# Bias tables loaded during the mixer instead of at the start of attention, and the first head's tiles in other space, in a hybrid attention and RWKV layer

## Chip, cores and metric

The kernel runs on one core of one Trainium2 chip. The metric is device microseconds of one execution. The core has a matrix engine (TensorE, PE in the profile, with its weight loads as PEld), VectorE (DVE), ScalarE (ACT), GpSimd (POOL) and SyncE (SP), and 16 DMA engines that move data between HBM and the on-chip memories SBUF (128 partitions) and PSUM. DMAs are issued by an engine's queue: SPq, ACTq or POOLq in the rows.

## What is computed

One layer of a trunk over 2048 tokens of width 1024. Three token mixers read columns of one projection of the normalised input: A is attention in chunks of 64 frames with a learned relative-position bias (4 heads), B is forgetting attention (4 heads), C is an RWKV-7 recurrence (8 heads). Their outputs are concatenated, projected and added; a gated feed-forward network follows. The part that the change touches is A:

```python
rel = kj - LEFT_CHUNKS * CHUNK - qi
bias = rel_table[:, jnp.clip(rel, -MAX_REL, MAX_REL) + MAX_REL].astype(jnp.float32)
...
    s = jnp.einsum('bhqd,bhkd->bhqk', qc, kb).astype(jnp.float32) + bias
    s = jnp.where(valid, s, NEG_INF)
    p = jax.nn.softmax(s, axis=-1).astype(vb.dtype)
    return jnp.einsum('bhqk,bhkd->bhqd', p, vb)
```

## The kernel before

The work runs in stages, one behind the other: the mixer (0 to about 1195 us), attention A and B (to about 1620 us), the output projection, and the feed-forward network (to 3254 us).

**The mixer** goes over four blocks of 512 tokens (`b` in `range(NB)`), each in four steps `i`. `project` multiplies the normalised input, whose tiles are `hT`, with slices of the weights (lines 268 to 270); `rwkv_front`, `rwkv_inverse` and `rwkv_back` compute the recurrence and are woven with it by generators. The inverse is a run of short VectorE instructions on `T` and `tm` (lines 520, 523), followed by small transfers through DRAM (`iD`, `E`, `DT`) on SP's queue. The recurrence reads `LZ` and the running state `S` in matmuls at lines 639 and 640. Queries and keys are written to `qkD` in DRAM as two halves `qh` and `ql` (lines 691, 692). For each block the last step of the recurrence loads `bv` (line 667), GpSimd adds it to `yl` (line 668), VectorE adds a PSUM tile (line 671), and GpSimd issues the store to `yD`. During block 1, `bias_rows` writes the relative biases, spread out, to `extD` and `exttD` in DRAM.

**Attention** goes over units: one head and one block of 512 queries. `shift` finds each query's largest score: for each of the four 128-query tiles matmuls write the scores to the PSUM tile `s` (lines 982, 987; there is one such tile), VectorE adds the bias table `TS` and takes the maximum (`sj`, line 991, with the read of the maximum as a second row), the four maxima are transposed (line 1012), and written into rows of `Q2` (line 1013). `attend` then computes transposed scores `st` with two matmuls (line 1043 with `Q1`, line 1044 with `Q2`, which needs the maxima), adds the table `TR` (line 1052), takes the exponential (line 1055) and multiplies with the values (line 1061). The shifts of units 0 and 1 stand ahead of the first `attend`; from then on the shift of unit u+2 is woven into `attend` of unit u.

`head` issues the loads of keys (`K1`, `K2`, lines 942 to 944) and values (`VA`, line 950) on SP, `queries` those of the queries (lines 959 to 961), for the first four units on ACT's queue (`QQ`). `bias` prepares the two tables of one head. It stands at the start of attention, and its loads are issued on ACT's queue (`BQ`), `TS` at line 904 and `TR` at line 906. Two constant tiles are made there too: `caub`, a cast of the loaded `cauf`, and `nid`.

The order in which an engine works is fixed when the program is built: a scheduler merges the generators' instructions for each engine, and an engine does not step past an instruction that waits. Each DMA on the queues of SP and ACT takes the next of eight completion counters, `DMAHW0` to `DMAHW7`, in turn, and is issued only when the DMA eight places earlier, which had the same counter, has landed.

Space in SBUF is given out by pools, as stacks from the left and from the right (`side="right"`). A tile that lies where an earlier stage's tile lay waits for that tile's last reader. Before, the right side begins with `hTp` (the `hT` tiles), then `xtp`, and after the mixer with `hd0` (head 0's keys), `qp` and `sm`, so the first keys lie over `hT`.

Of the kernel before, what the change touches and what calls it, by code (L numbers as in the profile page):

```python
# [48 lines left out]
PSB = {"m": 3, "f": 2, "b": 2}  # L49
# [48 lines left out]
def trunk_kernel(ctx: ExitStack, tc: tile.TileContext, xT, w_in, pp, cst, cau, rel, relr, w2, a2, g2, w_out, w_up, w_down, out, dbg=None):  # L98
# [39 lines left out]

    def copy(e, out, in_):
        e.copy(out, in_) if e is nc.scalar else e.tensor_copy(out=out, in_=in_)  # L140
# [6 lines left out]
    p1 = ExitStack()  # L147
    hTp = p1.enter_context(tc.tile_pool(name="hTp", bufs=1, side="right"))
    xtp = p1.enter_context(tc.tile_pool(name="xtp", bufs=1, side="right"))
# [6 lines left out]
    lzp = p1.enter_context(tc.tile_pool(name="lzp", bufs=NR0))  # L156
# [20 lines left out]
    nc.sync.dma_start(out=cst1, in_=cst[:, 256:NCC])  # L177

# [663 lines left out]
    for b in range(NB):  # L842
# [4 lines left out]
        for i in range(4):  # L847
            res = {}
            if b == 0 and i == 0:
                late.pop()()  # L850
                weave((), fill(b, hT, PRE))
            fills[:] = [fill(b, hT, jobs[i])]
            weave(
                (back, inv),
                lora_in(hT, lo) if i == 0 and b else (),
                rwkv_front(b, i, hT, lo, res),
                prepare(b + 1, xs) if i == 2 and b + 1 < NB else (),
                fills[0],
            )
            back, inv = (rwkv_back(prev) if prev else None), rwkv_inverse(res)  # L860
            prev = res
            if b == 1 and i == 1:
                bias_rows()
    weave((back, inv), fill(b, hT, LAST[4]))
# [8 lines left out]
    hd0 = p2.enter_context(tc.tile_pool(name="hd0", bufs=1, side="right"))  # L873
    qp = p2.enter_context(tc.tile_pool(name="qp", bufs=1, side="right"))
    sm = p2.enter_context(tc.tile_pool(name="sm", bufs=3, side="right"))
# [6 lines left out]
    cA = pA.enter_context(tc.tile_pool(name="cA", bufs=1, side="right"))  # L882
# [14 lines left out]

    TS = cA.tile([P, 4, 640], F32, name="TS")
    TR = cA.tile([P, 4, 256], F32, name="TR")

    def bias(h, q):

        a = extD[h].rearrange("q j -> (q j)")[127 : 127 + P * (EXT - 1)]
        q.dma_start(out=TS[:, h, :], in_=a.rearrange("(q j) -> q j", q=P)[:, 0:640])
        a = exttD[h].rearrange("q j -> (q j)")[127 : 127 + P * (EXTT - 1)]
        q.dma_start(out=TR[:, h, :], in_=a.rearrange("(q j) -> q j", q=P)[:, 0:256])
        nc.gpsimd.memset(TS[0:64, h, 576:640], NEG)
        nc.gpsimd.memset(TS[64:128, h, 0:64], NEG)
        nc.vector.tensor_scalar(TR[:, h, :], TR[:, h, :], par("rel0", h), None, op0=ALU.subtract)
        nc.gpsimd.memset(TR[64:128, h, 0:64], NEG)  # L910


    NQ = 4
    KVs, Qs = [], []
    for r, hd in enumerate((hd0, hd1)):
# [5 lines left out]
        nc.gpsimd.memset(f(K2[64:68, :]), 1.0)  # L921
        nc.gpsimd.memset(VA[:, :, 64:128], 1.0)
        nc.gpsimd.memset(f(V[:, :, 64:128]), 1.0)
        KVs.append((K1, K2, VA, V, VL))
    for r in range(NQ):
        Q1 = qp.tile([P, TB], F32R, name=f"Q1{r}")
        Q2 = qp.tile([70, TB], F32R, name=f"Q2{r}")
        QM = qp.tile([70, TB], F32R, name=f"QM{r}")
        for q in (Q2, QM):
            nc.gpsimd.memset(f(q[64:70, :]), 1.0)  # L930
        nc.gpsimd.memset(f(QM[64:68, :]), 0.0)
        Qs.append((Q1, Q2, QM))
# [89 lines left out]
    nid = c2.tile([4, 4, 1], F32, name="nid")  # L1022
    nc.vector.tensor_scalar(nid[:, :, 0], ident[0:4, 0:4], -1.0, None, op0=ALU.mult)
# [82 lines left out]
    bias(0, BQ(nc))  # L1106
# [8 lines left out]
    for h in range(1, 4):  # L1115
        bias(h, BQ(nc))
# [347 lines left out]
```

## Time and profile before

| what | us |
|---|---|
| median of 3 runs | 3266.54 |
| the 3 runs | 3254.4, 3266.54, 3267.34 |
| profiled execution | 3256.01 |
| its span, first to last instruction | 3254.2 |

The profiled execution is one run with the profiler on; rows below are from it, and their times count from its first instruction. PE is busy 93% of the span. PEclk is the granted clock of TensorE as a share of its full speed of 2.4 GHz, so 0.50 is 1.2 GHz. "DMA share" is the mean busy share of the 16 DMA engines (it can pass 1 in a short window, since packets are counted where they end). In brackets at the end of a timeline row stands how long the engine sat idle before it and what ended that.

### The profile page before, as it was taken

What the parts mean: (1) busy time and instruction counts of PE and PEld (TensorE: products, weight loads), DVE (VectorE), ACT (ScalarE), POOL (GpSimd) and SP (SyncE); (2) the same over time, 40 slices, a digit from 0 to 9 for tenths busy, and PEclk for the clock granted to TensorE, in tenths of its full rate; (3) what the DMA queues carried; (4) which work ended last, traced back from release to release, by engine and by line L of the source; (5) the groups of instructions that cost most, each with busy time, mean ns of one, the idle gap of its engine ahead of it and who ended that gap; (6) DMA issues with size and microseconds to landing.
All of it is one profiled execution on the core that took longest, in us unless ns stands there. A gap on an engine that the chain in (4) does not pass through costs nothing.

```text
span 3254.2 us, 49317 instructions
## 1 busy us (share of the span) xinstructions
PE 3037.6 (93%) x17820; PEld 2650.9 (81%) x17820; DVE 2373.9 (73%) x4569; ACT 1399.3 (43%) x2610; POOL 1000.3 (31%) x949
## 2 busy tenths in 40 slices
PE   6888899999999979999999999999899999999999
PEld 4567777776777755667699899999799998899999
DVE  5666666766677645677644688889988889988886
ACT  5343444434444334578733333333333334333332
POOL 3221001001000020144433444444544444444442
PEclk8888899999999987999999999999999999999999
DMA  7555665655653565532224422222422222422221
GB/s 222 148 166 170 175 181 163 190 149 157 162 161 101 169 152 141 141 99 77 76 90 148 143 79 78 78 78 74 154 74 77 78 78 81 140 78 78 78 79 67
DMA packets 440228, 392.94 MB, mean 121 GB/s; under 512 B 138809, under 2 KB 365637, under 8 KB 438633
## 3 DMA queue, kind: packets, MB, share of 16 engines
q1 hardware_dynamic: 435056, 377.99, 39.7%
q0 software_dynamic: 2816, 8.39, 0.9%
q10 hardware_dynamic: 2112, 3.41, 0.5%
q8 instruction: 141, 2.31, 0.3%
q14 instruction: 103, 0.84, 0.1%
HBM read 304.65 MB, written 86.36 MB: 120 GB/s over the span
## 4 chain that ended last, share of the span: by engine, by line
PE 66%; DVE 18%; issue 5%; ACT 4%; DMA 4%; POOL 2%; SPq 1%; POOLq 0%; ACTq 0%; DVEq 0%
PE ps L1291 7%; PE ps L1290 7%; PE ps L1289 7%; PE ps L1337 4%; PE ps L1335 4%; PE ps L1336 4%; PE mm L268 3%; PE mm L270 3%; PE mm L269 3%; DVE T L523 2%; PE o L1061 2%; DVE tm L520 2%; DVE wu L144 2%; PE z L639 2%; PE ps L1197 2%
## 5 line engine op out<-in xcount | busy, mean ns | idle before, releaser
L1291 PE MATMUL ps<-B,wu 128*128 128x340 f32 (+1 forms) x1848 | 593.2, 321 | 20.0 <-DVE wu L144 20.0
L1290 PE MATMUL ps<-B,wu 128*128 128x340 f32 (+1 forms) x1848 | 592.0, 320 | 0.0
L1289 PE MATMUL ps<-B,wu 128*128 128x340 f32 (+1 forms) x1848 | 589.4, 319 | 2.5 <-ACT wu L143 1.7
L1291 PEld LDWEIGHTS ps<-B,wu 128*128 128x128 f32 x1848 | 348.0, 188 | 27.6 <-DVE wu L144 27.2
L1335 PE MATMUL ps<-hid,wd 128*128 128x340 f32 (+1 forms) x1056 | 342.1, 324 | 14.3 <-ACT wd L143 10.2
L1289 PEld LDWEIGHTS ps<-B,wu 128*128 128x128 f32 x1848 | 347.9, 188 | 3.2 <-ACT wu L143 2.0
L1290 PEld LDWEIGHTS ps<-B,wu 128*128 128x128 f32 x1848 | 348.6, 189 | 0.1
L1337 PE MATMUL ps<-hid,wd 128*128 128x340 f32 (+1 forms) x1056 | 339.9, 323 | 3.1 <-POOL wd L144 3.0
L1336 PE MATMUL ps<-hid,wd 128*128 128x340 f32 (+1 forms) x1056 | 339.9, 322 | 0.0
L144 DVE TENSOR_TENSOR wu<-S,wu 128x512 fp32r<-128x512 f32 x264 | 257.0, 978 | 74.7 <-ACT wu L143 74.7
L1338 DVE TENSOR_TENSOR acc<-acc,ps 128x340 f32<-128x340 f32 (+1 forms) x528 | 248.3, 503 | 52.9 <-PE ps L1337 52.2
L144 POOL TENSOR_TENSOR wd<-raw,wd 128x1024 fp32r<-128x1024 f32 x66 | 171.0, 2613 | 277.3 <-ACT wd L143 272.9
L268 PE MATMUL mm<-hT,whi 128*128 128x512 f32 x520 | 235.9, 454 | 18.0 <-ACT whi L143 12.8
L270 PE MATMUL mm<-hT,wlo 128*128 128x512 f32 x520 | 220.3, 424 | 10.4 <-POOL wlo L144 6.4
L143 ACT CAST wu<-S 128x512 fp32r<-128x512 f32 x264 | 163.1, 619 | 150.5 <-PE ps L1291 137.9
L269 PE MATMUL mm<-hT,whi 128*128 128x512 f32 x520 | 219.3, 422 | 4.9 <-DVE hT L144 3.9
L1335 PEld LDWEIGHTS ps<-hid,wd 128*128 128x128 f32 x1056 | 201.8, 191 | 18.0 <-ACT wd L143 11.0
L144 DVE TENSOR_TENSOR wu<-raw,wu 128x512 fp32r<-128x512 f32 x198 | 203.0, 1026 | 6.4 <-ACT wu L143 6.4
L1337 PEld LDWEIGHTS ps<-hid,wd 128*128 128x128 f32 x1056 | 200.2, 190 | 5.5 <-POOL wd L144 5.5
L1336 PEld LDWEIGHTS ps<-hid,wd 128*128 128x128 f32 x1056 | 201.2, 190 | 0.0
L143 ACT CAST wu<-raw 128x512 fp32r<-128x512 f32 x198 | 121.5, 620 | 165.3 <-PE ps L1291 147.4
L268 PEld LDWEIGHTS mm<-hT,whi 128*128 128x128 f32 x520 | 105.5, 203 | 49.5 <-ACT whi L143 13.6
(348 smaller groups left out, 7140.4 us busy)
## 6 DMA issues: line engine op xcount, KB each, us to landing
raw<-in_w_up_dram SPq DMA_DIRECT2D x132, 512.0 KB
raw<-in_w_down_dram SPq DMA_DIRECT2D x66, 512.0 KB
whi<-whiD SPq DMA_DIRECT2D x48, 512.0 KB
wlo<-wloD SPq DMA_DIRECT2D x48, 512.0 KB
wraw<-in_w_in_dram SPq DMA_DIRECT2D x24, 512.0 KB
whiD<-whi SPq DMA_DIRECT2D x24, 512.0 KB
wloD<-wlo SPq DMA_DIRECT2D x24, 512.0 KB
xt<-in_xT_dram SPq DMA_DIRECT2D x48, 256.0 KB
```

The lines of the kernel that those rows point to most:

```text
L143: (hi_eng or nc.scalar).copy(hi, src) if (hi_eng or nc.scalar) is nc.scalar else hi_eng.tensor_copy(out=hi, in_=src)
L144: (lo_eng or nc.vector).tensor_tensor(lo, src, f(hi), op=ALU.subtract)
L268: mm(ps, hi[:, kt, 0:P], hT[kt][:, 0, :], start=(kt == 0), stop=False)
L269: mm(ps, hi[:, kt, 0:P], hT[kt][:, 1, :], start=False, stop=False)
L270: mm(ps, lo[:, kt, 0:P], hT[kt][:, 0, :], start=False, stop=(kt == KT - 1))
L1289: mm(ps, whl[:, 0, kt, :], Bs[p][:, kt, 0, 0:n], start=(kt == 0), stop=False)
L1290: mm(ps, whl[:, 0, kt, :], Bs[p][:, kt, 1, 0:n], start=False, stop=False)
L1291: mm(ps, whl[:, 1, kt, :], Bs[p][:, kt, 0, 0:n], start=False, stop=(kt == 3))
L1335: mm(ps, wd[:, 0, ch], hid[:, 0, cs], start=(u == 0), stop=False)
L1336: mm(ps, wd[:, 0, ch], hid[:, 1, cs], start=False, stop=False)
L1337: mm(ps, wd[:, 1, ch], hid[:, 0, cs], start=False, stop=(u == G - 1))
L1338: nc.vector.tensor_tensor(acc[ct][:, cs], acc[ct][:, cs], ps, op=ALU.add)
```

## The change

`bias` and its two tables move up. The tables lie in a pool `cA` that exists for the whole kernel, and `bias(i, nc.sync)` runs at the end of each step of block 2, so that its two loads for head `i` are issued on SP's queue, its memsets on GpSimd and its subtraction on VectorE somewhere during that block. The space (4 x 896 floats, 14,336 bytes in each partition) comes out of the scratch memory for DMA descriptors, which shrinks from its default of 16,384 to 2,048 bytes. The right side now begins with `xtp` and `lzp` (the `LZ` tiles), so head 0's keys and the queries lie over those; `hT` comes third, and `va` and `prA` lie over it. The PSUM pools of the mixer are opened in another order. GpSimd's memsets of ones are reordered, with those that the first units don't read in a function `ones`. `nid` is made at the start.

```diff
-PSB = {"m": 3, "f": 2, "b": 2}
+PSB = {"f": 2, "m": 3, "b": 2}
...
+    cA = ctx.enter_context(tc.tile_pool(name="cA", bufs=1))
+    TS = cA.tile([P, 4, 640], F32, name="TS")
+    TR = cA.tile([P, 4, 256], F32, name="TR")
+    nid = const.tile([4, 4, 1], F32, name="nid")
+
+    def bias(h, q):
+
+        a = extD[h].rearrange("q j -> (q j)")[127 : 127 + P * (EXT - 1)]
+        q.dma_start(out=TS[:, h, :], in_=a.rearrange("(q j) -> q j", q=P)[:, 0:640])
+        a = exttD[h].rearrange("q j -> (q j)")[127 : 127 + P * (EXTT - 1)]
+        q.dma_start(out=TR[:, h, :], in_=a.rearrange("(q j) -> q j", q=P)[:, 0:256])
+        nc.gpsimd.memset(TS[0:64, h, 576:640], NEG)
+        nc.gpsimd.memset(TS[64:128, h, 0:64], NEG)
+        nc.vector.tensor_scalar(TR[:, h, :], TR[:, h, :], par("rel0", h), None, op0=ALU.subtract)
+        nc.gpsimd.memset(TR[64:128, h, 0:64], NEG)
...
+    xtp = p1.enter_context(tc.tile_pool(name="xtp", bufs=1, side="right"))
+    lzp = p1.enter_context(tc.tile_pool(name="lzp", bufs=NR0, side="right"))
     hTp = p1.enter_context(tc.tile_pool(name="hTp", bufs=1, side="right"))
-    xtp = p1.enter_context(tc.tile_pool(name="xtp", bufs=1, side="right"))
...
-    lzp = p1.enter_context(tc.tile_pool(name="lzp", bufs=NR0))
...
                 bias_rows()
+            if b == 2:
+                bias(i, nc.sync)
...
     hd0 = p2.enter_context(tc.tile_pool(name="hd0", bufs=1, side="right"))
+    sm = p2.enter_context(tc.tile_pool(name="sm", bufs=3, side="right"))
     qp = p2.enter_context(tc.tile_pool(name="qp", bufs=1, side="right"))
-    sm = p2.enter_context(tc.tile_pool(name="sm", bufs=3, side="right"))
...
-    cA = pA.enter_context(tc.tile_pool(name="cA", bufs=1, side="right"))
...
-        Qs.append((Q1, Q2, QM))
+        Qs.insert(0, (Q1, Q2, QM))
+    nc.gpsimd.memset(f(KVs[0][1][64:68, :]), 1.0)
+    for Q1, Q2, QM in Qs:
+        nc.gpsimd.memset(f(Q2[64:70, :]), 1.0)
+    nc.gpsimd.memset(KVs[0][2][:, :, 64:128], 1.0)
+
+    def ones():
+        nc.gpsimd.memset(f(KVs[1][1][64:68, :]), 1.0)
...
-    bias(0, BQ(nc))
...
-    for h in range(1, 4):
-        bias(h, BQ(nc))
+    ones()
...
-    nc = _bacc.Bacc("TRN2", target_bir_lowering=False, num_devices=1)
+    nc = _bacc.Bacc("TRN2", target_bir_lowering=False, num_devices=1, dynamic_dma_scratch_size=2048)
```

Lines of the mixer move by 20 with the change, those of attention by 11 to 21 (the keys' loads 942 to 944 are 955 to 957, the values' 950 is 963, `sj` 991 is 1004, `st` 1043 and 1044 are 1054 and 1055; `TS` and `TR` 904 and 906 are 149 and 151).

**SP's queue at the end of the mixer.** This is the queue from the last store of the mixer's forget gates (`ckD`) on. A wait on `DMAHW` is one for an earlier DMA, one on `PE` for the last matmul that read the tile below. Before:

```order
L748 DMA ckD<-cl 4x512 [waits DMAHW0_49,DVE_49]
L691 DMA qkD<-qh 128x512 [waits DMAHW1_49,Activation_49]
L692 DMA qkD<-ql 128x512 [waits DMAHW2_49,DVE_49]
L942 DMA K_11077<-qkD 64x512 [waits DMAHW4_49,PE_49]
L943 DMA K_11077<-qkD 64x512 [waits DMAHW6_49]
L944 DMA K_11078<-qkD 64x512 [waits DMAHW7_49]
L942 DMA K_11077<-qkD 64x512 [waits DMAHW1_49]
L943 DMA K_11077<-qkD 64x512 [waits DMAHW2_49]
L667 DMA bv<-bD 128x512 [waits DVE_49,DMAHW4_49,PE_49,Pool_49]
L893 DMA cauf<-in_cau_dram 128x256 [waits DMAHW5_49,DVE_49,PE_49]
```

and of the change, from the same store (five more `DMA` rows stand between it and `bv` than before):

```order
L955 DMA K_11103<-qkD 64x512 [waits DMAHW4_49]
L956 DMA K_11103<-qkD 64x512 [waits DMAHW5_49]
L711 DMA qkD<-qh 128x512 [waits DMAHW6_49,Activation_49]
L712 DMA qkD<-ql 128x512 [waits DMAHW7_49,DVE_49]
L963 DMA VA_11105<-vA 128x4x64 [waits DMAHW1_49,PE_49]
L957 DMA K_11104<-qkD 64x512 [waits DMAHW3_49]
L963 DMA VA_11105<-vA 128x4x64 [waits DMAHW4_49]
L955 DMA K_11103<-qkD 64x512 [waits DMAHW6_49]
L956 DMA K_11103<-qkD 64x512 [waits DMAHW7_49]
L687 DMA bv<-bD 128x512 [waits DVE_49,DMAHW1_49,PE_49,Pool_49]
L914 DMA cauf<-in_cau_dram 128x256 [waits DMAHW2_49,DVE_49,PE_49]
```

The five loads of head 0's first keys (the last two of them are the first rows here) have moved ahead of the last stores of `qh` and `ql`, and their `PE` wait is for the last matmul that reads `LZ` instead of the last that reads `hT`. Two loads of values and three more of keys have moved ahead of `bv`. The `DMAHW1` that `bv` waits for is the counter of the first `VA`.

**VectorE at the same place.** Before, from the end of the mixer to the second unit's shift:

```order
L894 CAST caub<-cauf 128x256 [waits DMAHW5_49]
L909 TENSOR_SCALAR TR<-TR,pps 128x256 [waits DMAHW7_49,DMAHW2_49]
L671 TENSOR_TENSOR yl<-yl,rw 128x512 [waits DMASW6_49,Pool_49]
L991 ISA sj,M<-s,TS 128x128 [waits DMAHW3_49,PE_49,Pool_49]
...
L1013 SCALAR_TENSOR_TENSOR Q_11094<-s,pps,nid 4x512 [waits PE_49]
L909 TENSOR_SCALAR TR<-TR,pps 128x256 [waits DMAHW5_49]
L991 ISA sj,M<-s,TS 128x640 [waits DVE_49,PE_49,Pool_49]
```

and of the change:

```order
L1004 ISA sj,M<-s,TS 128x384 [waits PE_49]
L1004 ISA M 128x1
L162 TENSOR_TENSOR ql<-rn,qh 128x512 [waits DMAHW6_49,DMAHW7_49,DMAHW3_49,Activation_49]
L1004 ISA sj,M<-s,TS 128x512 [waits PE_49]
L1004 ISA M 128x1
L1026 SCALAR_TENSOR_TENSOR Q_11123<-s,pps,nid 4x512 [waits PE_49,Pool_49]
L691 TENSOR_TENSOR yl<-yl,rw 128x512 [waits DMASW6_49,Pool_49]
L915 CAST caub<-cauf 128x256 [waits DMAHW2_49]
L1004 ISA sj,M<-s,TS 128x640 [waits DVE_49,PE_49]
```

The first shift (`sj` up to the write of `Q`) has moved ahead of `yl` and `caub`, and `sj` no longer waits for the load of a table or for GpSimd's memsets on it. The second shift still stands behind `yl`, which waits for GpSimd's sum with `bv`, and `caub`.

**SP's queue in block 2 of the mixer.** Of the change, with the loads of the inverse (`iD`) at the end:

```order
L271 DMA wraw<-whiD_512_2401 128x4x256 [waits DMAHW1_49,PE_49]
L151 DMA TR<-exttD 128x256 [waits DMAHW2_49]
L149 DMA TS<-extD 128x640 [waits DMAHW3_49]
L271 DMA whi<-whiD_2564_605 128x8x128 [waits DMAHW4_49,PE_49]
...
L149 DMA TS<-extD 128x640 [waits DMAHW3_49]
L151 DMA TR<-exttD 128x256 [waits DMAHW4_49]
L149 DMA TS<-extD 128x640 [waits DMAHW5_49]
L548 DMA iD<-T 256x1x32 [waits DMAHW6_49,DVE_49,Pool_49]
```

Here six of the eight new loads stand between the weights' loads, one `TS` stands earlier and one `TR` later; before, none stood there. On VectorE the first subtraction on `TR` (line 154) stands within the run of `T` and `tm`:

```order
L543 TENSOR_TENSOR T<-T,tm 128x5x15 [waits DVE_49]
L154 TENSOR_SCALAR TR<-TR,pps 128x256 [waits DMAHW2_49]
L540 TENSOR_TENSOR tm<-T,NT 128x70 [waits DVE_49]
```

It waits for the `TR` load of the row above, and all of VectorE's later work stands behind it.

## Rows read from the trace of the kernel before

**Rows 1.** The page of before: section 1, busy us of the engines.
```profile
PE 3037.6 (93%) x17820; PEld 2650.9 (81%) x17820; DVE 2373.9 (73%) x4569; ACT 1399.3 (43%) x2610; POOL 1000.3 (31%) x949
```
**Rows 2.** Windows, mixer's end: busy us by engine, PEclk, DMA share, GB/s.
```profile
1180.00:1190.00 10.00, 9.82 (x52) 7.42 (x51) 5.71 (x13) 4.14 (x9) 0.00 (x0) 1.00 0.02 5
...
1200.00:1205.00 5.00, 0.00 (x0) 0.00 (x0) 0.76 (x1) 0.00 (x0) 2.12 (x2) 0.50 1.06 258
...
1220.00:1225.00 5.00, 3.06 (x5) 1.19 (x6) 3.21 (x9) 1.36 (x3) 0.44 (x3) 0.50 1.08 224
...
1240.00:1245.00 5.00, 5.00 (x14) 3.25 (x13) 1.34 (x5) 1.50 (x5) 0.29 (x2) 0.50 0.00 0
```
**Rows 3.** The chain that ended last: start us, us, what.
```profile
1192.16 3.35 DMA qkD<-ql
...
1195.53 7.26 DMA K<-qkD
...
1219.98 9.06 DMA TR<-exttD
```
**Rows 4.** DMA view of 1185 to 1245 us: packets; issues, KB each.
```profile
DMA packets 8730, 9.87 MB, mean 164 GB/s; under 512 B 4916, under 2 KB 5556, under 8 KB 8536
...
TS<-extD ACTq DMA_DIRECT2D x4, 320.0 KB
...
TR<-exttD ACTq DMA_DIRECT2D x4, 128.0 KB
```
**Rows 5.** Timeline, 1186 to 1235 us: start, us, instruction, [idle before].
```profile
1186.62 0.62 PE L639 MATMUL z<-UV,LZ 128*128 128x64 f32 x4
...
1192.63 0.57 SPq L942 DMA_DIRECT2D K<-qkD  x1
...
1196.47 0.33 SPq L667 DMA_DIRECT2D bv<-bD  x1
...
1203.82 1.25 POOL L668 TENSOR_TENSOR yl<-yl,bv 128x512 f32<-128x512 f32 x1 [2.88 <-DMA bv<-bD]
...
1204.24 0.98 DVE L894 CAST caub<-cauf 128x256 bf16<-128x256 f32 x1 [7.01 <-DMA cauf<-in_cau_dram]
...
1206.18 0.67 DVE L671 TENSOR_TENSOR yl<-yl,rw 128x512 f32<-128x512 f32 x1
...
1210.63 0.14 POOL L907 MEMSET TS<- 64x64 f32 x1
1210.81 0.29 DVE L991 CUSTOM_DVE_ANT_0 sj<-s,TS 128x128 bf16<-128x128 f32 x1 [3.96 <-POOL TS L907]
...
1215.60 0.74 DVE L1013 SCALAR_TENSOR_TENSOR Q<-s,pps,nid 4x512 fp32r<-4x512 f32 x1 [0.47 <-PE s L1012]
...
1220.89 0.82 DVE L991 CUSTOM_DVE_ANT_0 sj<-s,TS 128x640 bf16<-128x640 f32 x1
...
1222.70 0.82 DVE L991 CUSTOM_DVE_ANT_0 sj<-s,TS 128x640 bf16<-128x640 f32 x1 [0.32 <-PE s L987]
...
1231.14 0.82 DVE L991 CUSTOM_DVE_ANT_0 sj<-s,TS 128x640 bf16<-128x640 f32 x1 [0.78 <-PE s L987]
...
1234.13 1.54 PE L1044 MATMUL st<-Q,K 68*128 68x512 f32 x4
```
**Rows 6.** Windows in the mixer, 620 to 660 us: columns as in group 2.
```profile
620.00:640.00 20.00, 18.57 (x129) 13.88 (x128) 15.40 (x53) 8.20 (x16) 0.00 (x0) 0.91 0.89 250
640.00:660.00 20.00, 19.04 (x93) 14.37 (x92) 15.05 (x56) 14.81 (x28) 0.73 (x5) 1.00 0.63 175
```
**Rows 7.** Timeline of the mixer: SyncE's queue and VectorE.
```profile
639.71 0.52 SPq L251 DMA_DIRECT2D whi<-whiD  x1
...
643.86 0.23 DVE L523 TENSOR_TENSOR T<-T,tm 128x70 f32<-128x70 f32 x1
```
**Rows 8.** Line L909 and line L1093, each from its own view.
```profile
L909 DVE TENSOR_SCALAR TR<-TR,pps x4: 349/353/1112, 1205.1 to 1229.1; 128x256 f32<-128x256 f32 x4
...
DMA to landing us min/median/max: 2.2/2.3/7.8
```

More of the change, by code (lines that the diff above doesn't have):

```diff
@@ L177, in trunk_kernel @@
     nc.sync.dma_start(out=cst1, in_=cst[:, 256:NCC])
+    nc.vector.tensor_scalar(nid[:, :, 0], ident[0:4, 0:4], -1.0, None, op0=ALU.mult)
     omu = c1.tile([P, 14], F32, name="omu")
@@ L894, in trunk_kernel @@
     nc.vector.tensor_copy(out=caub, in_=cauf)
[L898 to L910, printed above, removed]
     NQ = 4
@@ L920, in trunk_kernel @@
         VL = vb.tile([P, 16, 64], F32R, name=f"VL{r}")
-        nc.gpsimd.memset(f(K2[64:68, :]), 1.0)
-        nc.gpsimd.memset(VA[:, :, 64:128], 1.0)
-        nc.gpsimd.memset(f(V[:, :, 64:128]), 1.0)
         KVs.append((K1, K2, VA, V, VL))
@@ L928, in trunk_kernel @@
         QM = qp.tile([70, TB], F32R, name=f"QM{r}")
-        for q in (Q2, QM):
-            nc.gpsimd.memset(f(q[64:70, :]), 1.0)
-        nc.gpsimd.memset(f(QM[64:68, :]), 0.0)
-        Qs.append((Q1, Q2, QM))
+        Qs.insert(0, (Q1, Q2, QM))
[5 more added lines that the diff above has]
+        nc.gpsimd.memset(f(KVs[1][1][64:68, :]), 1.0)
+        nc.gpsimd.memset(KVs[1][2][:, :, 64:128], 1.0)
+        for Q1, Q2, QM in Qs:
+            nc.gpsimd.memset(f(QM[64:70, :]), 1.0)
+            nc.gpsimd.memset(f(QM[64:68, :]), 0.0)
+        for K1, K2, VA, V, VL in KVs:
+            nc.gpsimd.memset(f(V[:, :, 64:128]), 1.0)
     def head(n, c=0, parts=1):
@@ L1020, in shift @@
         )
-    nid = c2.tile([4, 4, 1], F32, name="nid")
-    nc.vector.tensor_scalar(nid[:, :, 0], ident[0:4, 0:4], -1.0, None, op0=ALU.mult)
     pending = collections.deque()
```

## The prediction

> **What bounds the kernel now.** The page comes first: PE is busy 3037.6 us, 93% of the span of 3254.2 [rows 1], so a change that leaves the matrix work as it is can win only from PE's idle time, 217 us in all. The windows show where a piece of it lies. Until 1190 us PE is busy 9.82 of 10 us; in 1200 to 1205 it does nothing, in 1220 to 1225 it works 3.06 of 5, and all of that at a granted clock of 0.50, which it still has in 1240 to 1245 [rows 2]. This is the passage from the mixer to attention. The DMA engines were idle before it (share 0.02) and full in it (1.06 to 1.08, 258 and 224 GB/s). The chain of waits says for what: a store of queries (3.35 us), keys (7.26 us), and last a `TR` table (9.06 us) [rows 3]. The DMA view gives its size: 9.87 MB in the passage, of which the bias tables are 4 x (320 + 128) KB = 1.83 MB [rows 4].
>
> The timeline shows how the engines hang on it [rows 5]. The first `sj` (1210.81) sat idle 3.96 us for GpSimd's memset on a `TS` table. The second shift runs from 1220.89; its last `sj` starts at 1231.14, though its first two are only 1.81 us apart, because a `TR` subtraction stands ahead on VectorE and its load is late. The first `st` matmul on the second unit's maxima starts at 1234.13. I take this matmul as the anchor: behind it the change leaves the work as it is, so the gain is what the anchor moves, less what the mixer pays.
>
> **The passage, worked out.** Three things are removed there: 1.83 MB of loads, the memsets, and four subtractions on VectorE, one of 1.11 us and the others near 0.35 [rows 8]. One thing moves: head 0's keys are now requested when the last matmul on `LZ` has ended, 1186.62 + 0.62 = 1187.2, instead of at 1192.63 [rows 5]. That alone does not start attention sooner, since the queries' load stays where it was on ACT's queue, beside the store at 1192.16. A lightly loaded transfer takes 3.35 us [rows 3], so the first shift can start near 1195.5. From the first `sj` to its write of `Q` it took 1210.81 to 1215.60 + 0.74, or 5.5 us; with four VectorE instructions of the mixer between, each taken like `yl` at 0.67, it ends near 1203.7.
>
> Then `yl` and `caub` are next on VectorE, and here a new order costs something. `bv` was issued at 1196.47 and GpSimd could use it at 1203.82, 7.35 us later. Now it stands behind the first `VA`, on whose counter it waits. That load goes out behind the store at 1192.16, near 1192.6. No row shows a 128 KB value load in such a lull; it takes between 3.35 and 7.26 us [rows 3], and I take 5, nearer the lull: `bv` is issued near 1197.5. It then needs between 3.35 and 9.06 us, and I take 6, under its own 7.35, since less is in flight: 1203.5. GpSimd's sum 1.25, `yl` 0.67 and `caub` 0.98 follow [rows 5], with small gaps: the second shift starts at 1206.6. `cauf` has landed by then.
>
> The second shift: three steps of 1.81 us, then 2.99 us from the last `sj` to the anchor (1231.14 to 1234.13), and two `TR` additions in between, taken as 1.2 us. That is 9.6 us, so the anchor falls at 1216.2 instead of 1234.13: **17.9 us gained**. All this is at half clock, as in the rows.
>
> Bounds: with 7.26 for `VA` and 9.06 for `bv` the anchor is 5.4 us later, a gain of 12.5. With 3.35 for both, `bv` is there at 1199.4 and the first shift is the later one; the second starts at about 1205.4, a gain of 19. If PE keeps its full clock, since it idles less, it saves up to half of what it worked at 0.50: of some 12 us of solid work around 1240, 6 would be left. That makes 25 the upper bound.
>
> The Trainium skill (DMA: Bandwidth & Descriptors, "Anatomy of one DMA — SWDGE (gpsimd) path") would price the bytes at 436e3 per us: 1.83 MB would be an estimated 4.2 us, half of the 8.2 that 224 GB/s give. The trace does not reach that rate: more than half of the packets here are under 512 B, and 258 GB/s at full share is the most in these rows. My sum uses neither price, only the durations above.
>
> **The mixer, worked out.** Eight loads are added to SP's queue in block 2, where DMA share is 0.89 (620 to 640) and 0.63 (640 to 660) [rows 6]. The bytes fit: the two windows moved 250 and 175 GB/s times 20 us, 8.5 MB, and all of block 2's tables are 1.83. SP's queue is only an issuer here. What can cost is VectorE, which is busy 15 of 20 us with the inverse, while PE is busy 18.6 to 19.0. Four subtractions of 0.353 us [rows 8] cost at most 1.4 us; their cover is VectorE's own slack, which I give no credit. The first of them stands beside `T` at 643.86, and its load goes out ahead of the weights that were issued at 639.71 [rows 7]: it lands in time unless it takes over 4.2 us. Taken as hidden; the bound is 9.06 - 4.2 = 4.9 us, since all VectorE's work stands behind it, and nothing on the other side is gained. GpSimd is idle there (0.00 and 0.73 of 20), so the memsets, 0.14 us for one [rows 5], cost nothing; without that cover twelve of them would be 1.7 us. **1.4 us paid**, between 0 and 6.
>
> Smaller scratch: it serves GpSimd's own stores. They land in 2.3 us by the median [rows 8], there is one per unit, so few are ever under way: no cost. The Trainium skill (SBUF — State Buffer, "SBUF size: 192, 224, or 256?") counts 16 KiB as reserved for these descriptors, and the change takes 14 of it; by that the risk would be stores that wait for room, on an engine that is off the chain. No run here shows it yet. The pools, the order of PSUM banks and `nid` change only who waits for whom at the passage, and that is in the order used above.
>
> **Sum.** 17.9 - 1.4 = 16.5 us off the profiled execution of 3256.01, whose span is 3254.2: 3239.5. The four executions shown are two near 3255 and two near 3267; their mean is 3261.1, 5.1 above the profiled one and 5.4 below the median of runs, 3266.54. I put the forecast by that mean: **3245**. Its own range is 3234 to 3256.
>
> **Rivals.**
> 1. The other transfers keep the passage full. Then its end moves only by the bytes removed and the earlier keys: 1.83 MB at 224 GB/s is 8.2 us, and of the 5.4 us little counts if the queries' order decides. Gain 10, less 1.4: **3252**. For it: share above 1 up to 1225; against it: the last loads there are head 1's, which nobody waits for yet.
> 2. The passage closes further: `bv` early and the clock kept. Gain 24: **3237**. For it: PE idles less. Against: 0.50 is granted already in 1200 to 1205, right behind a short idle time.
> 3. The other sign: the table loads take places in the eight counters ahead of the inverse's transfers in block 2, and `iD`, on SP behind three of them, goes out late; the recurrence of the next step then waits, PE with it. One late load of 9.06 us is 5 us of stall; six of them in a row at 9.06, less the cover of 4.2 each, are 29 us. From 18 us of stall on it decides the sign; with all eight, 39 us, the time is **3282**. Against it: before, the weights' loads went through the same ring [rows 7], and PE stayed busy 18.6 of 20 us.
> 4. It doesn't do what it says: the passage is set by something that stays, such as the values or the second unit's queries, and the second shift starts no sooner than 1218. Gain 1: **3260**.
>
> **Chances.** Forecast 0.50, rival 1 0.18, rival 2 0.22, rival 3 0.06, rival 4 0.04. A measurement can tell about 0.5%, or 16.3 us, from no change, and the sum lies on that line: half of the forecast's chance and all of rival 2's are faster (0.47), the other half with rivals 1 and 4 is the same (0.47), rival 3 slower (0.06). The range takes in rivals 1 and 2 and the two levels of the runs: 3231 to 3258.
>
> **What would show it.** In the profile after: the first key load near 1187 to 1188; the first `sj` near 1196 and without a wait for GpSimd; GpSimd's sum with `bv` starting near 1203.5; the anchor (line 1055) near 1216, up to 2 later if block 2 is slower; no table in the chain. In block 2: four `TR` subtractions near 0.35 us and no wait of VectorE for a `TR` load over 1 us. Wrong would be: a start of `bv` later than 1206, queries that land after 1198, or stalls of VectorE or SP in block 2 above 5 us.

## The result, and the profile after

| what | us |
|---|---|
| before, median of 4 runs | 3260.95 (3254.4 to 3267.34) |
| after, median of 4 runs | 3236.31 (3229.11 to 3242.02) |
| ratio, after to before | 0.9922 (0.9897 to 0.9947) |
| profiled execution of after, its span | 3239.16, 3237.0 |

The change takes 24.6 us off, 0.8%, which is beyond the half per cent that tells from no change. The time lies in the predicted range, 8.7 us under the forecast of 3245 and next to the second rival's 3237. On the page of the profile after, PE's work is the same to 3 us, and it idles 202 us instead of 217 [rows 1].

```profile
PE 3034.8 (94%) x17820; PEld 2651.6 (82%) x17820; DVE 2371.9 (73%) x4569; ACT 1397.6 (43%) x2610; POOL 1001.1 (31%) x949
```

The mixer's last projection matmul starts at 1206.54 in this execution; before, it was at 1191.45. That is not the change: three profiles of the changed kernel have it at 1195.76, 1202.80 and 1206.54, two of the kernel before at 1191.45 and 1200.25. So from here on times of the passage count from this matmul ("after the mixer's end"). The windows after (columns as in [rows 2]) show the passage:

```profile
1205.00:1210.00 5.00, 3.13 (x12) 1.63 (x10) 3.38 (x6) 3.44 (x8) 2.95 (x6) 1.00 0.64 220
1210.00:1215.00 5.00, 3.02 (x11) 1.37 (x11) 3.62 (x11) 1.43 (x3) 4.94 (x7) 1.00 1.00 206
1215.00:1220.00 5.00, 1.30 (x4) 0.77 (x5) 1.73 (x3) 0.00 (x0) 2.72 (x5) 0.54 1.07 283
1220.00:1225.00 5.00, 4.80 (x13) 3.43 (x14) 3.51 (x10) 1.35 (x4) 2.48 (x4) 0.50 0.97 261
1225.00:1230.00 5.00, 5.00 (x10) 2.27 (x10) 1.41 (x4) 0.08 (x1) 0.00 (x0) 0.50 1.10 217
1230.00:1235.00 5.00, 4.50 (x16) 3.06 (x15) 3.10 (x8) 2.20 (x4) 0.00 (x0) 0.75 1.06 191
1235.00:1240.00 5.00, 5.00 (x23) 3.12 (x21) 3.32 (x9) 2.69 (x9) 1.08 (x5) 1.00 0.88 173
```

No window is without PE work now. The granted clock still falls to 0.50 (1.2 GHz), after a stretch in which PE worked 3.02 and then 1.30 of 5 us; but it is back at 1.00 at 1235, 29 us after the mixer's end. Before, it was still 0.50 in 1240 to 1245 [rows 2], which is 49 to 54 us after, and came back in the window behind it (first row below). That is not the same in every execution of the change: in its second profile, where the mixer ends at 1202.8, it comes back only in 1240 to 1245 (the other rows). The DMA engines are as full as before.

```profile
1245.00:1250.00 5.00, 5.00 (x16) 2.47 (x15) 1.97 (x5) 1.50 (x5) 0.00 (x0) 0.74 0.42 122
...
1235.00:1240.00 5.00, 5.00 (x16) 3.68 (x15) 1.09 (x3) 1.93 (x6) 0.29 (x2) 0.50 0.00 0
1240.00:1245.00 5.00, 5.00 (x15) 2.35 (x14) 2.42 (x7) 1.04 (x3) 0.00 (x0) 0.78 0.59 184
```

The chain of waits (columns as in [rows 3]) has no table any more. Where a store of queries, keys and a table stood, one transfer stands now, the load of the second unit's queries:

```profile
1207.63 1.14 PE mm L702 x2
...
1209.93 0.35 PE s L995
...
1210.91 6.19 DMA Q<-qkD
1217.24 0.87 PE s L1000 x2
```

The DMA view of 1200 to 1260 us answers to [rows 4]. The row of `TS` and that of `TR` are gone, and yet the bytes are not fewer, because other transfers have moved up into the 60 us:

```profile
DMA packets 10320, 10.04 MB, mean 167 GB/s; under 512 B 6982, under 2 KB 7110, under 8 KB 10122
```

The timeline answers to [rows 5]:

```profile
1202.35 0.48 SPq L955 DMA_DIRECT2D K<-qkD  x1
...
1210.32 0.29 DVE L1004 CUSTOM_DVE_ANT_0 sj<-s,TS 128x128 bf16<-128x128 f32 x1 [1.03 <-PE s L995]
...
1212.99 0.34 SPq L687 DMA_DIRECT2D bv<-bD  x1
...
1215.33 0.74 DVE L1026 SCALAR_TENSOR_TENSOR Q<-s,pps,nid 4x512 fp32r<-4x512 f32 x1 [0.43 <-PE s L1025]
...
1217.24 0.87 PE L1000 MATMUL s<-K,Q 64*128 64x320 f32 x2 [2.01 <-DMA Q<-qkD]
...
1217.72 1.25 POOL L688 TENSOR_TENSOR yl<-yl,bv 128x512 f32<-128x512 f32 x1 [2.16 <-DMA bv<-bD]
...
1219.01 0.69 DVE L691 TENSOR_TENSOR yl<-yl,rw 128x512 f32<-128x512 f32 x1 [2.93 <-POOL yl L688]
...
1220.20 0.81 DVE L1004 CUSTOM_DVE_ANT_0 sj<-s,TS 128x640 bf16<-128x640 f32 x1
...
1222.92 0.82 DVE L1004 CUSTOM_DVE_ANT_0 sj<-s,TS 128x640 bf16<-128x640 f32 x1 [0.82 <-PE s L1000]
...
1224.75 0.82 DVE L1004 CUSTOM_DVE_ANT_0 sj<-s,TS 128x640 bf16<-128x640 f32 x1 [0.45 <-PE s L1000]
...
1227.58 0.82 DVE L1004 CUSTOM_DVE_ANT_0 sj<-s,TS 128x640 bf16<-128x640 f32 x1 [2.00 <-PE s L1000]
...
1232.54 0.91 PE L1055 MATMUL st<-Q,K 68*128 68x512 f32 x4
```

The keys go out 4.2 us before the mixer's end, and the first `sj` waits for the scores alone, no more for GpSimd. The anchor, now line 1055, stands 26.0 us after the mixer's end; it was 42.7 [rows 5].

In the mixer the four subtractions (view of line 154) follow one another on VectorE without an idle row before any of them:

```profile
L154 DVE TENSOR_SCALAR TR<-TR,pps x4: 341/345/354, 648.8 to 681.4; 128x256 f32<-128x256 f32 x4
```

Every profile taken in this study is in the table below. The three columns next to the mixer's end are read from the timeline and count from it: the write of `Q` for the second unit, the anchor, and the last `yo` of attention. "At 0.50" is how long the granted clock was 0.50 between the anchor and attention's end, by the clock's own record in the trace, of which the PEclk of a window is the mean. The next column is from attention's end to the end of the span. The ratio is to runs of the kernel before on the same chip.

| kernel | mixer's end | second `Q` | anchor | attention's end | at 0.50 | attention's end to the end | ratio |
|---|---|---|---|---|---|---|---|
| before | 1191.5 | 41.1 | 42.7 | 427.1 | 30.6 | 1635.7 | |
| before, again | 1200.2 | 39.3 | 40.9 | 424.1 | 28.6 | 1636.9 | |
| after | 1206.5 | 23.6 | 26.0 | 401.4 | 10.2 | 1629.1 | 0.9922 (0.9897 to 0.9947) |
| after, again | 1202.8 | 22.9 | 25.4 | 405.8 | 24.3 | 1628.1 | |
| after, third | 1195.8 | 24.1 | 26.0 | 399.7 | 6.8 | 1630.9 | 0.9899 (0.9875 to 0.9923) |
| tables alone | 1201.0 | 27.5 | 29.2 | 410.0 | 24.2 | 1634.3 | 0.9925 (0.9901 to 0.9949) |
| tiles and memsets alone | 1203.9 | 36.2 | 38.9 | 423.7 | 31.0 | 1631.1 | 0.9985 (0.9971 to 1.0000) |
| memset order alone | 1192.3 | 34.1 | 36.2 | 415.2 | 18.0 | 1635.6 | 0.9953 (0.9938 to 0.9969) |
| `nid` alone | 1197.3 | 40.6 | 42.2 | 427.9 | 34.2 | 1632.8 | 0.9998 (0.9982 to 1.0014) |
| change, loads once more | 1193.0 | 22.9 | 31.4 | 400.5 | 7.3 | 1632.6 | 0.9894 (0.9865 to 0.9923) |
| change, `bv` on GpSimd | 1206.4 | 25.9 | 28.4 | 410.4 | 27.8 | 1629.5 | 0.9896 (0.9859 to 0.9933) |
| change, `bv` early | 1192.9 | 23.7 | 26.1 | 409.4 | 31.7 | 1629.3 | 0.9901 (0.9871 to 0.9931) |
| same, second queries on SP | 1195.6 | 23.2 | 24.8 | 401.7 | 19.6 | 1628.6 | 0.9917 (0.9894 to 0.9939) |

Attention's end moves by 3 to 6 us between executions of one kernel, so smaller differences in that column say nothing. Most of that movement is the clock: with the anchor at the same place, the three profiles of the change take 375.4, 380.4 and 373.7 us from the anchor to attention's end, and 10.2, 24.3 and 6.8 us of them at 0.50. The same holds across kernels. From the anchor to attention's end they take 373.7 to 385.7 us; less half of the time at 0.50, all take 367 to 370. (The kernel with the loads once more is left out here, since its anchor has other work ahead of it.)

### The profile page after: what moved, and what is told of

The parts are those of the page before. It is cut to its first block, busy times and chain, and to the rows that moved or that the text cites. A ratio compares the mean times of both kernels' runs of the same rounds, so it can differ in the third digit from the quotient of the medians.

```text
span 3237.0 us, 49300 instructions
## 1 busy us (share of the span) xinstructions
PE 3034.8 (94%) x17820; PEld 2651.6 (82%) x17820; DVE 2371.9 (73%) x4569; ACT 1397.6 (43%) x2610; POOL 1001.1 (31%) x949
## 4 chain that ended last, share of the span: by engine, by line
PE 69%; DVE 17%; issue 5%; ACT 5%; DMA 3%; POOL 2%; SPq 1%; POOLq 0%; ACTq 0%; DVEq 0%
PE ps L1300 7%; PE ps L1299 7%; PE ps L1298 7%; PE ps L1344 4%; PE ps L1345 4%; PE ps L1346 4%; PE mm L288 3%; PE mm L290 3%; PE mm L289 3%; PE o L1072 2%; DVE T L543 2%; DVE tm L540 2%; PE z L659 2%; PE ps L1206 2%; PE ps L1207 2%
## 5 line engine op out<-in xcount | busy, mean ns | idle before, releaser
L1300 PEld LDWEIGHTS ps<-B,wu 128*128 128x128 f32 x1848 | 348.5, 189 | 28.4 <-DVE wu L162 28.0
L1344 PE MATMUL ps<-hid,wd 128*128 128x340 f32 (+1 forms) x1056 | 341.1, 323 | 13.3 <-ACT wd L161 10.2
L288 PE MATMUL mm<-hT,whi 128*128 128x512 f32 x520 | 234.5, 451 | 15.2 <-ACT whi L161 10.8
```

Source lines behind the costliest of these rows:

```text
L288: mm(ps, hi[:, kt, 0:P], hT[kt][:, 0, :], start=(kt == 0), stop=False)
L1300: mm(ps, whl[:, 1, kt, :], Bs[p][:, kt, 0, 0:n], start=False, stop=(kt == 3))
L1344: mm(ps, wd[:, 0, ch], hid[:, 0, cs], start=(u == 0), stop=False)
```

## The experiments

### Both kernels once more

One execution of each, to see what a profile says of itself.

> The kernel before once more, for a second profile of the same program. Two readings of why the mixer ended 15 us later in the profile after (last projection matmul at 1206.5 instead of 1191.5 us): if it belongs to the change, the second profile of before has that matmul within 2 us of 1191.5; if executions of one program differ by that much, it lies 5 us or more away.

> The changed kernel once more. If the late end of the mixer belongs to the change, the last projection matmul is again within 2 us of 1206.5; if it is a matter of the execution, it lies 5 us or more away. The passage from that matmul to the anchor (the first score matmul on the second unit's maxima) is 26 us again under both, within 2 us, since its order and its loads are the same.

They took 3263.04 and 3238.84 us, beside a median of 3259.12 in 14 other runs of the kernel before. The mixer's end differs by 8.8 and 3.7 us from that of the first profiles; the passage is the same to 2 us.

### The tables alone, and the rest alone

The first kernel is that of before with its tables moved to block 2 and the smaller scratch; pools, memsets and `nid` stay.

```diff
+            if b == 2:
+                bias(i, nc.sync)
...
-    bias(0, BQ(nc))
...
-    for h in range(1, 4):
-        bias(h, BQ(nc))
```

> The tables move to block 2 of the mixer and the scratch shrinks; pools, memsets and PSUM order stay as before. My theory, that the tables' loads, memsets and subtractions are most of the gain in the passage: passage of 28 to 32 us (42.7 before, 26.0 after), time 3240 to 3250. The rival, that the first keys' earlier start over other tiles is most of it: passage above 36 us, time above 3253.

The second is the changed kernel with `bias` back at the start of attention on ACT's queue, its tables in the old space, and the scratch as before.

> Pools, memsets, PSUM order and the place of the small constant tile as in the change; the tables are loaded at the start of attention as before, on ScalarE's queue, and the scratch is as before. My theory: the first row maximum still waits for the table and the second shift for a subtraction, passage above 38 us, time 3254 to 3262. The rival: the earlier keys bring most of it, passage below 33 us, time below 3248. If the mixer's later end comes from the tiles' places, it shows here too: last projection matmul 10 us or more behind that of the second profile of before.

The tables alone give 0.9925, as much as the whole change within the intervals, and bring the anchor from 41.9 (mean of before, before again and `nid` alone) to 29.2. The rest alone gives 0.9985 and brings it to 38.9. In this second kernel the first `sj` comes 13.1 us after the mixer's end instead of 19.4, but half of that is lost again by the anchor. The groups of VectorE's instructions in 1190 to 1250 us (busy us, mean ns, then idle us before them and what ended it) show where:

```profile
L914 DVE TENSOR_SCALAR TR<-TR,pps 128x256 f32<-128x256 f32 x4 | 1.4, 358 | 9.5 <-DMA TR<-exttD 9.4
```

VectorE stands 9.4 us before the `TR` subtractions; the same group of the kernel before stands 9.2:

```profile
L909 DVE TENSOR_SCALAR TR<-TR,pps 128x256 f32<-128x256 f32 x4 | 2.2, 542 | 9.2 <-DMA TR<-exttD 9.2
```

So the tables bring the gain. That the earlier keys add to it is not shown: the rest brings the anchor 3.0 us forward by itself and 3.2 us on top of the tables (29.2 to 26.0), and the time shows no more than the 5 us, 0 to 9 by its interval, of the rest alone.

### Bytes, or waits for the tables?

The tables took three things out of the passage: transfers of 1.83 MB, the memsets on GpSimd's queue, and subtractions at which VectorE waits. To put back the first alone, the changed kernel issues the eight loads once more, at their old places on ACT's queue, into tiles that nobody reads.

```diff
+    def again(h, q):
+        a = extD[h].rearrange("q j -> (q j)")[127 : 127 + P * (EXT - 1)]
+        q.dma_start(out=TSd[:, h, :], in_=a.rearrange("(q j) -> q j", q=P)[:, 0:640])
+        a = exttD[h].rearrange("q j -> (q j)")[127 : 127 + P * (EXTT - 1)]
+        q.dma_start(out=TRd[:, h, :], in_=a.rearrange("(q j) -> q j", q=P)[:, 0:256])
...
     queries(*units[0], QQ(nc))
+    again(0, BQ(nc))
...
+    for h in range(1, 4):
+        again(h, BQ(nc))
```

> The change, with the eight table loads issued once more at the start of attention, at the old places on ScalarE's queue, into a tile that nobody reads: 1.83 MB of transfers come back to the passage, without any memset, subtraction or wait for a table. The passage is 24.4 us in the change. If the transfers themselves (bytes, and the queue and counters that they take) made most of the loss, it grows to 32 us or more and the time by 8 us or more. If it was the waits of VectorE and GpSimd for the tables, the passage stays below 28 us and the time within 4 us of the change.

Measured: 0.9894 (0.9865 to 0.9923), where the change beside it on the same chip took 0.9899. The DMA view of 1187 to 1247 us shows the loads in the passage, slow ones (13.0 us from issue to landing for the first table, by the median):

```profile
DMA packets 11370, 11.71 MB, mean 195 GB/s; under 512 B 7084, under 2 KB 7724, under 8 KB 11173
...
TSd<-extD ACTq DMA_DIRECT2D x4, 320.0 KB, 13.0
...
TRd<-exttD ACTq DMA_DIRECT2D x4, 128.0 KB
```

The write of `Q` for the first unit is 4 us later than in the change (13.0 after the mixer's end instead of 8.8 to 9.0), that for the second is not (22.9). The anchor is at 31.4, since in this build the scores of the third unit stand ahead of it on PE; attention ends at 400.5, where the change ends at 399.7 to 405.8. So the transfers and their places on the queue cost nothing that shows at the end of attention; by the time alone, four runs of each would leave room for some 8 us. What cost before was that somebody waited for the tables.

### Which wait: GpSimd's memsets, or the late loads?

The kernel before, with the order of GpSimd's memsets taken from the change and all else left: the ones that the first units don't read come last, behind the tables.

```diff
-        nc.gpsimd.memset(f(K2[64:68, :]), 1.0)
-        nc.gpsimd.memset(VA[:, :, 64:128], 1.0)
-        nc.gpsimd.memset(f(V[:, :, 64:128]), 1.0)
...
-        for q in (Q2, QM):
-            nc.gpsimd.memset(f(q[64:70, :]), 1.0)
-        nc.gpsimd.memset(f(QM[64:68, :]), 0.0)
...
+    nc.gpsimd.memset(f(KVs[0][1][64:68, :]), 1.0)
+    for Q1, Q2, QM in Qs:
+        nc.gpsimd.memset(f(Q2[64:70, :]), 1.0)
+    nc.gpsimd.memset(KVs[0][2][:, :, 64:128], 1.0)
...
+    ones()
```

> The kernel before with the change's order of GpSimd's memsets alone: the table's memsets come ahead of most of the ones. The second unit's maxima are written 40.3 us after the mixer's last matmul in before (mean of three profiles), 23.5 in the change, 27.5 with the tables moved alone. If the memsets ahead of the table held the second unit up, the write comes at 37 us or sooner and the time falls by 4 us or more. If the late TR loads with their subtractions on VectorE set it, only the first maximum moves (19.4 us after the mixer to about 15.5) and the write stays within 1.5 us of 40.3, the time within 3 us of before.

I had held the late `TR` loads for the cause and expected little; the rival held. The ratio is 0.9953 (0.9938 to 0.9969), and the timeline shows it:

```profile
1204.82 1.26 POOL L668 TENSOR_TENSOR yl<-yl,bv 128x512 f32<-128x512 f32 x1 [3.73 <-DMA bv<-bD]
...
1206.02 0.29 POOL L907 MEMSET TS<- 64x64 f32 x1
...
1206.75 0.38 DVE L909 TENSOR_SCALAR TR<-TR,pps 128x256 f32<-128x256 f32 x1
...
1207.05 0.27 DVE L998 CUSTOM_DVE_ANT_0 sj<-s,TS 128x128 bf16<-128x128 f32 x1
```

The first memset on `TS` starts 13.7 us after the mixer's end (before: 19.2, with memsets on `V`, `VA` and `QM` ahead of it), and the first `sj` no more waits for it. The second `Q` comes 6 us earlier than before, 4.6 of them at the first `sj`, and attention ends 11 us earlier, though VectorE still waits 7.5 us for the `TR` loads. Of the 16 us by which the tables alone bring attention's end forward, GpSimd's order alone gives back 11, about half of them up to the anchor and half behind it.

Two things limit this. VectorE's order moved with the edit: before, three `TR` subtractions stand between the two writes of `Q`; here two do, and the last comes behind the second write:

```profile
1226.38 0.74 DVE L1020 SCALAR_TENSOR_TENSOR Q<-s,pps,nid 4x512 fp32r<-4x512 f32 x1 [0.47 <-PE s L1019]
...
1228.97 0.35 DVE L909 TENSOR_SCALAR TR<-TR,pps 128x256 f32<-128x256 f32 x1 [1.85 <-DMA TR<-exttD]
```

And the rest alone has the same order of memsets and gained only 5 us (0.9985) where this kernel gained 15 (0.9953). Its first `sj` came even sooner, but VectorE then stood 9.4 us for `TR` loads, and the clock was at 0.50 for 31.0 us behind the anchor, against 18.0 here. So the memset was the first wait, but removing it pays in full only where the next one does not take its place.

### Does `bv` decide when the second shift starts?

The prediction put the second shift behind `bv`. First, the last `bv` is issued by GpSimd, past SP's queue.

```diff
-        nc.sync.dma_start(out=bv, in_=bD)
+        (nc.gpsimd if (b, i) == (NB - 1, 3) else nc.sync).dma_start(out=bv, in_=bD)
```

> The change, with the last load of bv issued by GpSimd instead of behind the values on SyncE's queue. If bv governs the second shift, as I forecast, the sum with bv starts 3 to 4 us sooner after the mixer's last matmul than the 10.9 us of the change, and the passage falls from 24.4 to about 21 us. The rival, that the second unit's queries govern it (they landed 10.6 us after that matmul): the sum starts sooner and the passage stays within 1 us.

The ratio is 0.9896, but it tells nothing of `bv`: behind GpSimd's memsets it went out 7.3 us after the mixer's end (change: 6.5) and was used at 11.8 (11.2). Then `bv` got a tile of another pool, free long before, so that it is loaded 33 us ahead of the mixer's end.

```diff
-        bv = t512("bv", "bp")
+        bv = t512("bv", "fr" if (b, i) == (NB - 1, 3) else "bp")
```

> The change, with the last bv loaded into a tile of another pool that is free long before, still by SyncE: the load is in by the mixer's end. If bv governs the second shift as I forecast, yl runs 5 us sooner than the 12.6 us after the mixer's last matmul and the second unit's maxima are written at 20 us or sooner instead of 23.5. If the second unit's queries govern it (landed 10.6 us after that matmul), the write stays above 22.5 us. The time is 1 to 4 us below the change in the first case and equal in the second.

The ratio is 0.9901, the same as the change. `yl` comes at 7.3 instead of 12.5 after the mixer's end, and the second `Q` at 23.7 as before. The timeline of this kernel, whose mixer ends at 1192.88:

```profile
1197.13 1.26 POOL L688 TENSOR_TENSOR yl<-yl,bv 128x512 f32<-128x512 f32 x1
...
1198.40 0.29 DVE L1004 CUSTOM_DVE_ANT_0 sj<-s,TS 128x128 bf16<-128x128 f32 x1 [4.28 <-PE s L995]
...
1204.78 0.74 DVE L1026 SCALAR_TENSOR_TENSOR Q<-s,pps,nid 4x512 fp32r<-4x512 f32 x1
...
1206.51 0.82 DVE L1004 CUSTOM_DVE_ANT_0 sj<-s,TS 128x640 bf16<-128x640 f32 x1 [0.99 <-PE s L1000]
```

GpSimd's sum runs at 1197.13, without a wait. But the first shift now starts 5.5 us after the mixer's end (change: 3.8) and takes 6.4 us from its first `sj` to its write of `Q` (change: 1210.32 to 1215.33, 5.0), with `yl` and other work of the mixer between on VectorE, and the second shift starts where it did, 13.6 us after. A last try moved the second unit's queries, for which PE waits in the change, from ACT's queue to SP's:

```diff
-    queries(*units[1], QQ(nc))
+    queries(*units[1], nc.sync)
```

> As bv_early, and the second unit's queries are loaded by SyncE, ahead of the second part of the keys, not by ScalarE behind its work on yl. If the two transfers together are what is left to wait for, the second unit's maxima are written 18 us after the mixer's last matmul or sooner (23.5 in the change), PE keeps its full clock longer, and the time is 4 to 8 us below the change. The rival, that the full DMA engines only hand the wait on to the next transfer: the write stays above 21 us and the time equals the change's.

The second `Q` is at 23.2, the ratio 0.9917 (0.9894 to 0.9939): nothing gained. The rival had said so, but for another reason, that full DMA engines hand the wait on to the next load. In both kernels PE waits at the second shift's first scores for the first shift's `Q`, and for no load (`bv` early, then second queries on SP):

```profile
1205.57 0.90 PE L1000 MATMUL s<-K,Q 64*128 64x320 f32 x2 [1.21 <-DVE Q L1026]
...
1207.30 0.90 PE L1000 MATMUL s<-K,Q 64*128 64x320 f32 x2 [0.83 <-DVE Q L1026]
```

With the loads out of the way it is the first shift, later and longer than in the change, that the second stands behind.

### `nid` alone

The kernel before with `nid` (4 x 4 numbers, 16 bytes in a partition) made at the start, in the pool `const`.

```diff
+    nid = const.tile([4, 4, 1], F32, name="nid")
...
+    nc.vector.tensor_scalar(nid[:, :, 0], ident[0:4, 0:4], -1.0, None, op0=ALU.mult)
```

> The kernel before, with the small constant tile nid (16 bytes in a partition) in the first pool and made at the start, nothing else. From the end of attention on the change takes 1628.6 us where before takes 1636.3, with the same order; bias_only has 1634.3, tiles_only 1631.1. If the shift of the later tiles by these bytes is the cause, this kernel takes 1631 us or less there, and in the down projection some 370 of the matmuls follow the one before by 161 to 200 ns, not some 745. If the cause is elsewhere in the tiles, it takes 1635 us or more and has 700 or more of those.

By time nothing that can be told: 0.9998 (0.9982 to 1.0014). But from attention's end to the end its profile takes 1632.8 us, 3 to 4 less than the kernel before, with the same instructions in the same order. In the table the nine profiles of kernels with `nid` in `const` have 1628.1 to 1632.8 there, the four others 1634.3 to 1636.9. The view of the down projection's third matmul line (min, median, max of its ns), first of before, then of this kernel:

```profile
L1337 PE MATMUL ps<-hid,wd x1056: 312/319/654, 1870.6 to 3249.8; 128*128 128x340 f32 x117, 128*128 128x344 f32 x59
```

```profile
L1339 PE MATMUL ps<-hid,wd x1056: 312/317/656, 1878.3 to 3253.6; 128*128 128x340 f32 x117, 128*128 128x344 f32 x59
```

Counted over the trace's rows of all three lines, 365 of its 3167 matmuls start 161 to 200 ns behind the one before and 2496 start 151 to 160 behind it; before, 731 and 759 are of the slower kind in the two profiles, 2155 and 2123 of the faster.

### The change a third time

> The changed kernel once more beside these, for a third profile and more times of it: 3236 within 4 us, passage 24 to 25 us, end of the mixer anywhere between 1192 and 1207 us, as executions of one program differ there.

It took 0.9899 (0.9875 to 0.9923) of the kernel before on its chip. The loads once more, `bv` on GpSimd and `nid` alone ran beside it and are read against this line; the memset order, `bv` early and the second queries on SP ran on another chip and have only their ratio to the kernel before there.

## Why the prediction was right, and where it was not

Times after the mixer's end; the forecast's are those of the prediction less 1191.45, the measured ones are of the first profile after.

| step | forecast | measured |
|---|---|---|
| first keys requested | -4.2 | -4.2 |
| first shift starts (its `s`) | 4.0 | 3.4 |
| first shift done | 12.2 | 9.5 |
| `bv` issued | 6.0 | 6.5 |
| `bv` used by GpSimd | 12.0 | 11.2 |
| first `sj` of the second shift | 15.1 | 13.7 |
| from there to the anchor | 9.6 | 12.3 |
| anchor | 24.8 | 26.0 |

**The passage: right in size.** 17.9 us were forecast; the mean anchor of the three profiles after is 25.8, that of the three with the tables and pools of before 41.9: 16.1 us. PE's idle time between the mixer's end and the anchor fell from 21 to 23 us to 7 to 8. The keys, the queries, the vanished wait for GpSimd and the empty chain came as the steps had it.

**Two steps in it were wrong and made up for each other.** "The second shift starts at 1206.6" was worked out behind `bv`; in the change `yl` does wait for it, but `bv` early left the second `Q` where it was, so `bv` is not the one that decides: the second unit's queries and the first shift's own length hold the second shift at about the same place. And "9.6 us" for the second shift was built from steps of 1.81 us and a last piece of 2.99; after, the steps are 2.72, 1.83 and 2.83 us, and the last piece 4.96, because products of the first unit stand between them on PE at half clock (the last `sj` waits 2.00 us for its scores). The rest of the passage, from 1220 to the anchor, is PE's: it works 4.80, 5.00 and 4.50 of 5 us there, at 0.50 for most of it, and the chain has no transfer behind 1217.10. What was not tried is the same passage at full clock.

**What the tables cost.** The prediction listed bytes, memsets and subtractions without saying which of them paid. It was the waits, first that for the `TS` memset behind other memsets on GpSimd, then those for the `TR` loads; the bytes paid nothing that shows, as the loads issued once more say. The first rival, that transfers keep the passage full and only bytes count, falls with that: the passage is as full as before and 16 us shorter. By the trace's rate the bytes were 8.2 us; here they did not cost that, since nobody waited for them. By the Trainium skill (DMA: Bandwidth & Descriptors, "Anatomy of one DMA — SWDGE (gpsimd) path") they were an estimated 4.2 us. The trace is below the page's rate: the windows with full DMA engines above moved 191 to 283 GB/s.

**The mixer: small, as forecast, but not where the forecast put it.** From the eighth to the thirteenth step's `kka` row, the stretch that holds block 2, the five profiles without table work there take 353.4 to 357.7 us, mean 355.3, the eight with it 355.2 to 358.8, mean 357.6: 2.2 us against 1.4. But the table work (603.6 to 682 us in the change) lies between the eighth and the tenth row, and there both take the same, 136.4 without it and 135.8 with it. The difference comes behind it, 219.0 and 221.8 us from the tenth to the thirteenth row. There PE has 10.9 us of its work at 0.50 without the table work and 15.2 with it, by the means; half of that difference is most of it. So no run shows the 1.4 us of the subtractions as a cost, and whether the tables or chance bring the lower clock stays open. The mixer's end is 1197.0 against 1199.2 by the same means, with spreads of 12 and 14 us. There is no wait for a `TR` load (the row of line 154), so the third rival, the other sign, did not come.

**The scratch: no cost, as forecast.** GpSimd's stores land as before [rows 8], by the view of line 1104:

```profile
DMA to landing us min/median/max: 2.2/2.3/6.5
```

The Trainium skill (SBUF — State Buffer, "SBUF size: 192, 224, or 256?") counts 16 KiB as reserved for these descriptors. With 14 of them given away this kernel shows no store that waits longer.

**What the sum lacked.** From the mixer's end to attention's end the kernel gained 24.1 us (mean 426.4 to 402.3), 16.1 of them up to the anchor, and from there to the end 6.9 (1636.3 of two profiles to 1629.4). Two terms are missing, then.

"Behind it the change leaves the work as it is" was the step that failed for the first: the work is the same, but not its clock, and behind the anchor 8.0 us more came back. The column "at 0.50" shows from where. Before, the clock is at 0.50 for 31.1 us between the anchor and attention's end (mean of the three profiles), and PE works through nearly all of them; after, for 13.8. Work at half the clock takes up to twice as long, so half of the difference would be given back: 8.7 us, where 8.0 were measured. I had this as an upper bound and as half of the second rival, whose other half, an early `bv`, gained nothing. That the clock costs this is shown by the three profiles of the one program; what lets it come back 25 to 26 us after the mixer's end in two of them and 39 in the other is not.

The second term is in the feed-forward network, whose work the change does not touch: by its one profile, `nid` alone brings some 3.5 of these 6.9 us, by the places of tiles; the rest stays open, and profiles of one kernel differ there by up to 2.8. With the mixer's 2.2 paid, 24.1 + 6.9 - 2.2 = 28.8 us; measured were 24.6, with an interval of 17 to 34.

So the passage was understood, but the sum of 16.5 us is a third short of what was measured. The time lies near the low end of the forecast's own range of 3234 to 3256, an end that had counted the clock; that the feed-forward network added a gain which no step had is luck.

## What to carry to other kernels

When a passage is full of transfers, ask of each not how many bytes it has, but which engine stands still for it and what is queued behind that engine: here the order of GpSimd's memsets, with a 0.14 us memset that `sj` waited for, brought 15 of some 25 us by itself, and 1.83 MB put back cost nothing that shows. The cheap half of such a change, the order of one queue, should be tried alone, and read in that kernel alone: beside the change's other tiles the same order brought 5 us. And when idle time goes, the matrix engine's clock can also come back sooner, so the work behind the passage must be in the sum, and the time at half clock should be read for every profile before two of them are compared.

## What the runs showed of the hardware that was not expected

The same instructions in the same order take the mixer 1191 and 1200 us in the two profiles of before, and 1196 to 1207 in the three of the change. The step that differs most is that between the `kka` rows of the fourteenth and the fifteenth step: 32.2 and 36.7 us before, and 36.7, 36.7 and 32.2 in the change. The windows of exactly this step, of the first profile before and the first after, show the same 160 matmuls and a different clock:

```profile
973.80:1005.98 32.18, 30.12 (x160) 22.98 (x160) 27.05 (x81) 14.32 (x30) 2.41 (x7) 1.00 0.28 69
...
981.68:1018.41 36.73, 34.65 (x160) 25.94 (x160) 27.13 (x81) 14.32 (x30) 2.41 (x7) 0.86 0.25 61
```

In all thirteen profiles the step follows the clock: 32.2 us where it stays at 1.00 (four profiles), 35.2 to 35.3 with 6.8 us at 0.50 (four), 36.7 with 10.2 (four), 39.4 with 17.1 (one). Over the whole mixer, too, the profiles that end early (1191 to 1193) have 110 to 114 us of PE's work at 0.50, and those that end at 1206 to 1207 have 138 to 140. Why one execution is granted the full clock where another is not, no run shows.

Sixteen bytes more in an early pool move the tiles behind it, and with that the share of slow starts in the down projection halves: 731 and 759 of 3167 in the two profiles of before, 764 with the tables alone; 365 with `nid` alone, 371, 370 and 363 in the three of the change. Which tile's place does it was not tried.
